# Pinning the first readers of the solved blocks behind the latest weights, and writing them ten units later

## The chip, the cores and the metric

The kernel runs on one core of a Trainium2 chip. The metric is the device time of one execution in microseconds (us); 2533.32 us is the median of three runs before the change (2533.11 to 2533.87).

## What is computed

Two transformer blocks over 256 tokens of width 2048, batch 1, all in float32. The first block has two mixers side by side: a gated delta rule (GDN, 8 heads of 128) and a block attention, which for 256 tokens is plain causal attention (8 heads of 128). Their outputs are gated, summed and projected, and a convolved gated feed-forward of width 5632 follows. The second block (two layers with modulation, sparse attention and retention) is not touched.

The change sits in the GDN. Cut to what matters, for each head:

```python
a_mat = where(strict, (k * beta) @ k.T * gamma, 0)     # per chunk of tokens
t_mat = triangular_solve(eye + a_mat, eye)             # unit lower triangular inverse
u = t_mat @ (v * beta)
w = t_mat @ (k * beta * exp(gc))
# scan over the chunks:
v_new = u - w @ state
o = (q * exp(gc)) @ state + (q @ k.T * gamma) @ v_new
state = state * exp(g_last) + kd.T @ v_new
```

The kernel uses two chunks of 128 tokens a head in place of the reference's chunks of 64, which gives the same output.

## The kernel before

**Weights.** All matrix products run in float32 split into a rounded high half and a low half (three matmuls a tile). Weights come in granules of 128 x 1024 (512 KB; 128 x 696 for the attention's value blocks). `load_w` (lines 215 to 227) issues the DMA of a granule on SP's queue (`w`, 4 buffers), rounds it on ACT into `wh` (line 222, 3 buffers) and takes the rest on DVE into `wl` (line 223, 4 buffers). A chunk of projection output (128 columns by 256 tokens) needs two granules, 48 matmuls. Between granules a side job issues a share of the modulation vector's products: a 256 KB DMA `mw` and one DVE instruction (line 1094), three for four granules.

**Who orders what.** TensorE's instructions run in the order in which the program writes them. For every other engine a planner fixes the order of its queue from priorities and its own cost estimates; each queue then runs strictly in that order. `behind()` (lines 230 to 234) is a means to hold the planner: what is written inside it comes, on its own engine, after the DMA, the ACT copy and the DVE subtraction of the granule loaded last.

**Tasks and the emission clock.** The work between the big products is written by generators (tasks). `self.clk` counts units of TensorE time: a matmul of 256 columns in the rounded format adds 0.107, one in plain float32 four times as much per column. After each triplet of weight matmuls `tick` advances the first task in the list whose time has come by one step; `yield 3.0` means "not before 3 units from now". `finish(t)` writes steps, always of the task that is due first, and moves the clock forward to it, until t is done: no weight matmuls come between these steps.

**The GDN.** Heads go in two groups of four. Per group (`mixers`, lines 589 to 628):
- key and query chunks of each head (`kq`, two buffers) and a task `gdn_scores`, which writes the head's blocks into a tile `gS`, two heads to a tile, three tiles in all;
- one task `gdn_solve` (line 785) once all four score tasks are done: POOL issues four DMAs that gather the 32 x 32 diagonal blocks in DRAM (`gD`, line 799), reads them as 32 partitions of 32 x 32 (`gX`, line 800), eliminates 30 columns with two POOL instructions each (lines 805 and 806), stores `gX`, and issues eight DMAs that put the blocks back into `gS` (line 810). The task yields 1.3 units a column and 8 after the last DMA, then sets `group.solved`;
- value and gate chunks, then a task `gdn` (line 814) for each head. It polls once a unit until `group.solved`; heads 2 and 3 of a group also wait for heads 0 and 1. Its first step reads the solved blocks on DVE (`level(0)`: `gbm`, line 829, and `DE`, line 834); 3.5 units later TensorE transposes `DE` (line 838); then two merging levels, the products with the values, the norm and the gate follow in about ten steps.

Forced finishes in group 1: heads 0 and 1 of group 0 are finished after the key and query chunks of head 6, since its tile `gS` is theirs (line 602). After group 1 come a value block of the attention (`a_block(2)`) and eight attention heads of two chunks each; the attention task of head h - 2 is finished before the chunks of head h (line 633).

Of the kernel before, what the change touches and what calls it, by code (L numbers as in the profile page):

```python
# [12 lines left out]
OP = mybir.AluOpType  # L13
# [24 lines left out]
def _consts():  # L38
# [37 lines left out]
    ret = {"rot": rot}  # L76
    dec = np.ascontiguousarray((dec * SC).astype(f).transpose(1, 0, 2, 3)).reshape(H, P, 2 * P)
    return base, gdn, ret, dec, lev


# [45 lines left out]
class Net:  # L126
# [386 lines left out]
    def mixers(self, bo, b1):  # L513
        nc, tmp, a = self.nc, self.tmp, self.a
        self.b1 = b1
        raw = self.side("v")
        ln1 = lambda k: self.col("ln1", k)

        def prep(k):
            if k == 1:  # L520
                nc.sync.dma_start(self.xg[0][:, 1:4], a["xT"][:, 1:4])
            if k == 8:
                nc.sync.dma_start(self.par[:, KT:], a["par"][:, KT:])
            if k % 4 == 2 and k < 12:
                g = k // 4 + 1
                nc.sync.dma_start(self.xg[g], a["xT"][:, 4 * g:4 * g + 4])
            if k == 12:
                nc.sync.dma_start(self.cst0, a["cst0"])
                nc.sync.dma_start(self.mod, a["bmod"])
                nc.sync.dma_start(self.row, a["row"].to_broadcast([P, 272]))  # L530
            self.raw(raw[k], k, ln1)
            self.sumsq(self.acc, self.x[k], k == 0)

        hs = self.side("u")
        nrm = {}

        vb = [b1.tile([P, 1024], F32, name=f"vb{tt}") for tt in range(2)]

        def a_block(b, scale):
            ps = self.gemm_a(a["wA1"][b], NA1, hs if b else raw, None if b else prep)  # L540
            if b == 0:
                nrm["task"] = self.add(self.normalize(0.0, [self.acc], self.one_norm, hs, ln1, out=nrm))
                while "col" not in nrm:
                    self.step(nrm["task"])
                scale = nrm["col"]
                self.add(self.gdn_gates(ps, scale))
            lo = b * NA1
            j0, j1 = max(lo, 16), min(lo + NA1, 1040)
            for tt in range(2):
                d, q = vb[tt][:, j0 - 16:j1 - 16], ps[tt][:, j0 - lo:j1 - lo]  # L550
                if b == 0:
                    nc.scalar.mul(d, q, scale[:, tt:tt + 1])
                else:
                    nc.scalar.copy(d, q)

        a_block(0, None)
        self.cst1 = b1.tile([P, CST1.shape[1]], F32, name="cst1")
        nc.sync.dma_start(self.cst1, a["cst1"])
        lev = self.pw.tile([P, 1024], F32, tag="w", name="levf", bufs=4)
        nc.sync.dma_start(lev[:, 0:3 * P], a["lev"])  # L560
        self.lev = b1.tile([P, 3 * P], mybir.dt.bfloat16, name="lev")
        nc.vector.tensor_copy(self.lev, lev[:, 0:3 * P])
        self.bo, self.hs = bo, hs
        self.mod_done, self.mod_ahead, self.pmo = 0, [], None
        self.job("mod", self.modulation(), 0)
        ci = 0

        def early():

            nonlocal ci  # L570
            ps = self.chunk(a["wB1"][ci], raw if ci < NRAW else hs)
            ci += 1
            if ci > NRAW:
                return ps
            t = tmp.tile([P, T], F32, tag="rt1", name="un", bufs=2)
            nc.vector.tensor_tensor(t, ps, nrm["row"][:, 0:T], op=OP.mult)
            return t

        def part(dst, j, h):
            ps = early()  # L580
            if j < 3:
                self.conv(dst, ps, lambda t: self.col("gconv", (j * 8 + h) * 4 + t), 4)
            nc.scalar.activation(dst, dst if j < 3 else ps, ACT.Silu)
            if ci == NRAW:
                self.finish(nrm["task"])
                o = self.side("v")
                self.oa, self.ob = o[0:8], o[8:16]

        groups = []
        for p in range(2):  # L590
            hh = range(4 * p, 4 * p + 4)
            group = Group(hh)
            S = []
            for i, h in enumerate(hh):
                kq = b1.tile([P, 2, T], F32, tag="kq", name="kq", bufs=2)
                for j, dst in ((1, kq[:, 0]), (0, kq[:, 1])):
                    part(dst, j, h)
                if i >= 2:
                    self.finish(group.scores[i - 2])
                if i % 2 == 0:  # L600
                    if p and i:
                        for t in groups[0].heads[:2]:
                            self.finish(t)
                    S.append(b1.tile([P, 2, 6, P], F32, tag="gS", name="gS", bufs=3))
                group.scores.append(self.add(self.gdn_scores(h, kq, S[i // 2][:, i % 2], group)))
            group.solve = self.add(self.gdn_solve(S, group))
            for i, h in enumerate(hh):
                v = b1.tile([P, T], F32, tag="v", name="v", bufs=1)
                if p and i >= 1:
                    self.finish(groups[0].heads[i - 1])  # L610
                z = b1.tile([P, T], F32, tag="z", name="z", bufs=5)
                part(v, 2, h)
                part(z, 3, h)
                if i >= 1:
                    self.finish(group.values[i - 1])
                group.values.append(self.add(self.gdn_values(h, v, group.scores[i], group)))
                group.z[h] = z
                if (p, i) == (0, 0):
                    self.mod_to(bo, RATE[0])
                if (p, i) == (0, 3):  # L620
                    with self.behind():
                        posf = self.pos_row(tmp, a["positions"], "sq")
                        cos, sin = self.trig(b1, posf, self.c1("rope"), "rope")
                    a_block(1, None)
            for i, h in enumerate(hh):
                group.heads.append(self.add(self.gdn(h, S[i // 2][:, i % 2], group, group.heads[i - 2:i - 1] if i >= 2 else
                                                     groups[-1].heads[2 + i:3 + i] if groups else [])))
            groups.append(group)
        a_block(2, None)
        mob = []  # L630
        for h in range(H):
            if h >= 2:
                self.finish(mob[h - 2])
            qk = b1.tile([P, 2, T], F32, tag="kq", name="qkb", bufs=2)
            for j in range(2):
                ps = self.chunk(a["wB1"][ci], hs)
                ci += 1
                self.rotate(qk[:, j], ps, cos, sin, 32)
            mob.append(self.add(self.moba(h, qk[:, 0], qk[:, 1], vb, self.ob[h])))
        self.mod_to(None, 0)  # L640
        self.sig = [self.gates(m) for m in range(4)]
        self.drain()
# [142 lines left out]
    def gdn_solve(self, S, group):  # L785


        nc, b1 = self.nc, self.b1
# [19 lines left out]
        nc.gpsimd.dma_start(Df, X)  # L808
        for d, y in diag:
            nc.gpsimd.dma_start(y, d)  # L810
        yield 8.0
        group.solved = True

    def gdn(self, h, S, group, before):
        nc, b1 = self.nc, self.b1
# [8 lines left out]
        idb = self.c0("ident").unsqueeze(1).to_broadcast([P, 2, P])  # L824

        def level(l):
            m = self.lev[:, l * P:(l + 1) * P].unsqueeze(1).to_broadcast([P, 2, P])
            bm = tl("bm", [P, 2, P])
            nc.vector.tensor_tensor(bm, B, m, op=OP.mult)
            return bm  # L830

        bm = level(0)
        DE = tl("DE", [P, 2, 2, P])
        nc.vector.tensor_tensor(DE[:, 1], idb, bm, op=OP.subtract)
        yield 3.5
        pd = self.aux([P, 2, P])
        for tt in range(2):
# [2 lines left out]
        for l in (1, 2):  # L840
            bm = level(l)
# [630 lines left out]
```

## Time and profile before

| what | value |
|---|---|
| median of three runs | 2533.32 us |
| profiled execution, its own time | 2533.55 us |
| its span | 2531.7 us |
| TensorE busy | 2454.0 us (97%), 20026 matmuls |
| DVE busy | 1905.9 us (75%) |
| ACT busy | 1391.4 us (55%) |
| POOL busy | 140.6 us (6%) |
| memory traffic, mean | 212 GB/s |

Busy TensorE time counts pipelined matmuls, so a share of 97% is no peak; where TensorE does not reach 9 tenths in a slice, something kept it waiting. The page's slices are 63 us each. The work spoken of here lies between 50 and 480 us.

### The profile page before, as it was taken

The page shows a single profiled execution, that of the slowest core. Times are in us where ns is not written, and L with a number is a line of the kernel's source. Part 1 is how long each engine was busy: PE and PEld are TensorE (multiplying, and loading weights), DVE is VectorE, ACT ScalarE, POOL GpSimd, SP SyncE. Part 2 cuts the span into 40 slices and gives each one's busy share as a digit, 9 for nine tenths or more (in the row PEclk, how much of TensorE's full clock was granted, in tenths as well). Part 3 has the DMA queues.
Part 4 walks back from the last instruction along what each step waited for, and adds up shares of the span by engine and source line. Part 5 has one row for each costly group of instructions (what it writes and reads, how often), then busy time and mean ns, then how long its engine had stood idle before and what let it go on. Part 6 is the DMA issues. An engine that isn't in the chain of part 4 may idle for free.

```text
span 2531.7 us, 50856 instructions
## 1 busy us (share of the span) xinstructions
PE 2454.0 (97%) x20026; PEld 2438.4 (96%) x20026; DVE 1905.9 (75%) x3673; ACT 1391.4 (55%) x2208; POOL 140.6 (6%) x215
## 2 busy tenths in 40 slices
PE   8959779999999999999999999999999999999999
PEld 8959779999999999999999999999999999999999
DVE  7747567667788988888877678898888677666664
ACT  7626446544444556777754456654844556475443
POOL 0341610000000000000000000000000000000000
PEclk9979989999999999999999999999999999999999
DMA  6545474588898766766767767768677555455555
GB/s 219 192 148 168 137 229 143 183 266 300 295 299 297 225 223 209 239 221 210 243 215 211 242 216 218 216 211 266 211 245 236 179 183 174 152 169 171 176 184 159
DMA packets 190224, 536.66 MB, mean 212 GB/s; under 512 B 22176, under 2 KB 27680, under 8 KB 189984
## 3 DMA queue, kind: packets, MB, share of 16 engines
q1 hardware_dynamic: 188768, 532.36, 65.5%
q8 instruction: 157, 2.57, 0.4%
q0 software_dynamic: 1216, 1.05, 0.2%
q14 instruction: 83, 0.68, 0.1%
HBM read 530.70 MB, written 2.62 MB: 211 GB/s over the span
## 4 chain that ended last, share of the span: by engine, by line
PE 89%; DVE 3%; POOL 3%; DMA 2%; issue 1%; ACT 1%; SPq 0%; DVEq 0%; ACTq 0%; POOLq 0%
PE mm L186 84%; PE aux L186 4%; POOL gX L806 2%; POOL gXt L805 1%; DVE wl L223 1%; PE aux L190 1%; ACT wh L222 1%; DVE mw L1094 0%; DVE isc L1304 0%; DMA gX<-gD 0%; DMA w<-wA 0%; DMA gD<-gS 0%; DMA mc<-c 0%; DMA gD<-gX 0%; DMA mw<-wM 0%
## 5 line engine op out<-in xcount | busy, mean ns | idle before, releaser
L222 ACT CAST wh<-w 128x1024 fp32r<-128x1024 f32 (+5 forms) x867 | 854.0, 986 | 938.0 <-PE mm L186 771.4
L186 PE MATMUL mm<-u,wh 128*128 128x256 f32 (+1 forms) x7488 | 1361.9, 284 | 0.0
L223 DVE TENSOR_TENSOR wl<-w,wh 128x1024 fp32r<-128x1024 f32 (+5 forms) x867 | 993.6, 1147 | 400.6 <-ACT wh L222 396.1
L186 PEld LDWEIGHTS mm<-u,wh 128*128 128x128 f32 x7488 | 1152.8, 189 | 3.3 <-issue 2.4
L186 PE MATMUL mm<-u,wl 128*128 128x256 f32 (+1 forms) x3744 | 1053.9, 281 | 51.7 <-DVE wl L223 51.7
L186 PEld LDWEIGHTS mm<-u,wl 128*128 128x128 f32 x3744 | 706.9, 189 | 52.1 <-DVE wl L223 52.1
L186 PE MATMUL mm<-v,wh 128*128 128x256 f32 (+1 forms) x4096 | 743.4, 283 | 0.0
L186 PEld LDWEIGHTS mm<-v,wh 128*128 128x128 f32 x4096 | 629.3, 189 | 1.4 <-issue 1.0
L186 PE MATMUL mm<-v,wl 128*128 128x256 f32 (+1 forms) x2048 | 576.2, 281 | 1.6 <-DVE wl L223 1.4
L186 PEld LDWEIGHTS mm<-v,wl 128*128 128x128 f32 x2048 | 385.8, 188 | 2.6 <-DVE wl L223 2.6
L1094 DVE CUSTOM_DVE_ANT_0 mw<-mw,mc,mod 128x512 f32<-128x512 f32 x192 | 145.0, 759 | 2.9 <-ACT mc L1076 2.1
L1094 DVE CUSTOM_DVE_ANT_0 mw<-mw,mc,part 128x512 f32<-128x512 f32 x192 | 142.2, 747 | 2.7 <-ACT mc L1076 2.7
L186 PE MATMUL mm<-wh,u 128*128 128x412 f32 (+1 forms) x320 | 83.4, 339 | 0.0
L1052 ACT ACTIVATE leaf<-bit,row,dr 128x384 f32<-128x384 f32 x120 | 78.9, 699 | 0.0
L186 PE MATMUL mm<-wh,v 128*128 128x412 f32 (+1 forms) x256 | 71.8, 359 | 5.7 <-ACT wh L222 5.7
L694 DVE SCALAR_TENSOR_TENSOR u<-mm,par,u 128x255 f32<-128x255 f32 (+1 forms) x160 | 76.4, 477 | 0.7
L335 POOL TENSOR_TENSOR rc<-rc,cst 128x2 f32<-128x2 f32 x4 | 3.7, 928 | 1296.2 <-DVE rc L388 1296.2
L186 PE MATMUL mm<-more,wh 128*128 128x256 f32 x384 | 69.8, 281 | 0.0
L186 PEld LDWEIGHTS mm<-more,wh 128*128 128x128 f32 x384 | 59.1, 189 | 0.0
L186 PEld LDWEIGHTS mm<-wh,u 128*128 128x128 f32 x320 | 58.3, 188 | 0.2
L186 PEld LDWEIGHTS mm<-wh,v 128*128 128x128 f32 x256 | 50.2, 200 | 6.8 <-ACT wh L222 6.6
L1056 DVE COPY_PREDICATED leaf<-bit,leaf 128x384 f32<-128x384 uint32 x88 | 53.5, 608 | 2.5 <-ACT leaf L1052 1.9
(297 smaller groups left out, 1996.2 us busy)
## 6 DMA issues: line engine op xcount, KB each, us to landing
w<-wB SPq DMA_DIRECT2D x344, 512.0 KB, 3.9
mw<-wM SPq DMA_DIRECT2D x384, 256.0 KB, 4.0
w<-wUp SPq DMA_DIRECT2D x170, 512.0 KB, 4.0
w<-wO SPq DMA_DIRECT2D x96, 512.0 KB, 4.2
w<-wDn SPq DMA_DIRECT2D x64, 384.0 KB, 3.6
w<-wDn SPq DMA_DIRECT2D x64, 320.0 KB, 3.5
w<-wA SPq DMA_DIRECT2D x48, 412.0 KB, 3.2
w<-wBr SPq DMA_DIRECT2D x32, 512.0 KB, 4.4
```

Of the source, the lines that this page charges most:

```text
L186: self.nc.tensor.matmul(out, l, r, start=start, stop=stop)
L190: self.nc.tensor.transpose(out, in_, self.c0("ident"))
L222: i1 = nc.scalar.copy(h[:, :n], w[:, :n])
L223: i2 = nc.vector.tensor_tensor(l[:, :n], w[:, :n], h[:, :n].bitcast(F32), op=OP.subtract)
L335: self.nc.gpsimd.tensor_tensor(out, in_, e, op=OP.pow)
L694: nc.vector.scalar_tensor_tensor(dst[:, s:], ps[:, :T - s], tap(width - 1 - s), dst[:, s:], op0=OP.mult, op1=OP.add)
L805: nc.gpsimd.tensor_tensor(t, col, row, op=OP.mult)
L806: nc.gpsimd.tensor_tensor(X[:, 0:j, j + 1:32], X[:, 0:j, j + 1:32], t, op=OP.subtract)
L1052: nc.scalar.activation(t, bits[0], ACT.Identity, scale=dr[:, i, h:h + 1], bias=rb[:, i, 0, h:h + 1])
L1056: nc.vector.copy_predicated(t, bits[l].bitcast(mybir.dt.uint32), u)
L1094: self.nc.vector.tensor_tensor_reduce(w, w, c, 1.0, src, OP.mult, OP.add, dst)
```

## The change

Three edits. The wait after the solve's last DMA grows from 8 to 18 units of the emission clock. The two DVE instructions of `level(0)` are written inside `behind()`. The finish of the score task of two heads earlier moves ahead of a head's `kq` tile and chunks, and is done for every head from the third on, across the two groups (before: after the chunks, for the third and fourth head of a group).

```diff
             for i, h in enumerate(hh):
+                if h >= 2:
+                    self.finish((groups + [group])[(h - 2) // 4].scores[(h - 2) % 4])
                 kq = b1.tile([P, 2, T], F32, tag="kq", name="kq", bufs=2)
                 for j, dst in ((1, kq[:, 0]), (0, kq[:, 1])):
                     part(dst, j, h)
-                if i >= 2:
-                    self.finish(group.scores[i - 2])
                 if i % 2 == 0:
...
         for d, y in diag:
             nc.gpsimd.dma_start(y, d)
-        yield 8.0
+        yield 18.0
         group.solved = True
...
-        bm = level(0)
         DE = tl("DE", [P, 2, 2, P])
-        nc.vector.tensor_tensor(DE[:, 1], idb, bm, op=OP.subtract)
+        with self.behind():
+            bm = level(0)
+            nc.vector.tensor_tensor(DE[:, 1], idb, bm, op=OP.subtract)
         yield 3.5
```

## Rows read from the trace of the kernel before

**Rows 1.** The page, busy tenths and granted clock in 40 slices of the span

```profile
PE   8959779999999999999999999999999999999999
PEclk9979989999999999999999999999999999999999
```

**Rows 2.** TensorE's waits, 0 to 420 us: total us, times, longest

```profile
PE mm L186 <- DVE wl L223: 53.4, 5, 26.4
```

**Rows 3.** Stretches: PE, PEld, DVE, ACT, POOL busy us; clock; DMA share; GB/s

```profile
134.67:161.06 26.39, 0.00 (x1) 0.01 (x1) 2.63 (x6) 0.45 (x1) 19.76 (x39) 0.54 0.05 10
161.06:165.00 3.94, 3.94 (x21) 3.94 (x22) 3.94 (x14) 0.18 (x1) 0.00 (x0) 0.61 0.48 157
165.00:181.50 16.50, 16.05 (x101) 15.54 (x100) 13.14 (x25) 9.01 (x16) 0.00 (x0) 1.00 0.82 266
...
225.25:234.09 8.84, 6.08 (x42) 4.58 (x40) 5.65 (x21) 6.19 (x19) 2.37 (x3) 1.00 0.38 124
...
303.20:328.51 25.31, 0.05 (x1) 0.00 (x0) 2.62 (x6) 0.87 (x2) 18.71 (x38) 0.58 0.06 10
...
374.90:385.00 10.10, 8.05 (x60) 7.09 (x59) 8.19 (x28) 6.86 (x20) 0.00 (x0) 1.00 0.45 148
```

**Rows 4.** Timeline of DVE: start, us, instruction, idle before and its releaser

```profile
158.43 0.76 DVE L829 TENSOR_TENSOR gbm<-gS,lev 128x256 f32<-128x256 f32 x2 [29.16 <-DMA gS<-gD]
159.78 1.22 DVE L223 TENSOR_TENSOR wl<-w,wh 128x1024 fp32r<-128x1024 f32 x1
...
188.40 1.23 DVE L223 TENSOR_TENSOR wl<-w,wh 128x1024 fp32r<-128x1024 f32 x1 [0.94 <-ACT wh L222]
...
325.89 0.76 DVE L829 TENSOR_TENSOR gbm<-gS,lev 128x256 f32<-128x256 f32 x2 [27.96 <-DMA gS<-gD]
```

**Rows 5.** Timeline of TensorE: weight matmuls behind the stall and later

```profile
161.43 0.63 PE L186 MATMUL mm<-u,wh 128*128 128x256 f32 x2
...
181.55 0.39 PE L186 MATMUL mm<-u,wh 128*128 128x256 f32 x2
...
181.90 0.40 PE L186 MATMUL mm<-u,wh 128*128 128x256 f32 x2
```

**Rows 6.** Timeline of POOL: the solve of group 0

```profile
109.81 0.87 POOL L805 TENSOR_TENSOR gXt<-gX 32x30 f32<-32x30 f32 x1 [3.92 <-DMA gX<-gD]
...
127.20 1.52 POOL L806 TENSOR_TENSOR gX<-gX,gXt 32x220 f32<-32x220 f32 x1
...
130.49 0.60 POOL L805 TENSOR_TENSOR gXt<-gX 32x234 f32<-32x234 f32 x1
...
138.92 0.59 POOL L805 TENSOR_TENSOR gXt<-gX 32x228 f32<-32x228 f32 x1
...
140.98 0.60 POOL L806 TENSOR_TENSOR gX<-gX,gXt 32x220 f32<-32x220 f32 x1
...
151.56 0.25 POOL L806 TENSOR_TENSOR gX<-gX,gXt 32x30 f32<-32x30 f32 x1
```

**Rows 7.** DMAs to landing: those of tile gX, then those of gS

```profile
DMA to landing us min/median/max: 2.3/3.3/4.4
...
DMA to landing us min/median/max: 1.7/1.9/3.7
```

**Rows 8.** Timeline of TensorE: GDN and attention steps

```profile
202.89 0.38 PE L190 MATMUL aux<-cst,gDE 128*128 128x128 f32 x2
...
205.13 0.95 PE L186 MATMUL aux<-cst,gsq 128*128 128x1 f32 x8
...
370.38 0.38 PE L190 MATMUL aux<-cst,gDE 128*128 128x128 f32 x2
...
374.91 0.82 PE L186 MATMUL aux<-qkb 128*128 128x128 f32 x4
...
442.43 0.82 PE L186 MATMUL aux<-qkb 128*128 128x128 f32 x4
...
451.29 1.65 PE L186 MATMUL aux<-spt,vb 128*128 128x128 f32 x6 [1.64 <-ACT spt L919]
```

## The prediction

> **What bounds the kernel now.** Read the 40 slices of the page first: TensorE is at 9 tenths almost everywhere, and the exceptions lie in the first 440 us, slices 3, 5 and 6 above all, with the granted clock down in the third and the sixth [rows 1]. The waits of TensorE in that stretch come next: one line holds nearly all of them, 53.4 us for the low halves of weights (wl, line 223), the longest 26.4 us [rows 2]. The stretches place it: TensorE does nothing in 134.67 to 161.06 and in 303.20 to 328.51, DVE next to nothing, while POOL works on [rows 3]. Then ask DVE what it stands at: line 829, the first reader of the solved blocks, idle 29.16 and 27.96 us until the DMA that writes the blocks back lands; the next wl runs only behind it [rows 4]. So these two stretches are bound by the solve on POOL, and only because a reader stands in DVE's queue ahead of weights that need nothing from it. The first TensorE work on that reader's result is at 202.89 and 370.38, more than 40 us later in the stream [rows 8]: nobody needs it where it stands.
>
> **The change, part by part.** Sums are against the profiled execution, 2533.55 us (its span 2531.7 and 1.85 around it), 0.23 over the median.
>
> *The pin.* Lines 829 and 834 at level 0 go behind the wl of the granule latest loaded when they are written. Where is that? The write of level 0 lies 3.5 units of the emission clock ahead of the transposes; a unit is 1.12 us of TensorE (a triplet of 256 columns counts 0.32 and takes 0.358, the step from 181.55 to 181.90 [rows 5]). So it lies at 202.89 - 3.9 = 199.0 and at 370.38 - 3.9 = 366.5. The pinned pair can't reach the wl of 134.67 or 303.20 any more. The level 1 reader writes the same buffer (gbm, one copy), so it stays behind line 834 without a pin. Both stalls go: 26.39 + 25.26 = 51.65 us. With them goes the slow restart: after 161 a triplet takes 0.64 instead of 0.358 at a granted clock of 0.61 [rows 3, 5], about 1.4 us until 164 (0.25 for the first, four at 0.28) and as much is taken after 328.5; and 0.45 us of idle at 165, where the window has 16.05 busy of 16.50. Gain: 51.65 + 2.8 + 0.45 = 54.9 us.
>
> *What is late next: the solve itself.* DVE was idle for the second half of it and won't be now. Twelve rounds beside a working DVE took 109.81 to 130.49, 20.7 us; the mirrored twelve, of the same sizes, beside an idle one 138.92 to 151.81, 12.9 us; the same 220-element subtraction is 1.52 and 0.60 [rows 6]. The ratio is 1.60. The 18 rounds left at 130.49 (21.3 us) become 34.2 and end at 164.7, in the denser attention block (DVE 80% busy at 165 to 181.5 [rows 3]) perhaps at 167. From there to the landed blocks it was 6.6 us (151.81 to 158.4); with both transfers at their slowest (4.4 for 2.3, 3.7 for 1.9 [rows 7]) 10.5. The blocks land between 171 and 178.
>
> The Trainium skill (SBUF — State Buffer, section Who interferes with whom) says that a DVE instruction with two SBUF inputs and a GpSimd instruction that reads SBUF exclude each other for a whole instruction; by that, with wl and modulation products both of that kind and DVE at 80%, the solve would crawl at a fifth of its speed until DVE stands still again. The trace agrees with the lock for single instructions (1.52 for 0.60), not with that share: 1.60 was measured beside a normal stream. Its result is the second rival.
>
> *The 18 for 8.* Ten units later is 11.2 us of TensorE: the write moves from 199.0 to about 210 and from 366.5 to 377.7 in the old stream. In both groups a forced finish comes first. For group 0 the head-6 block begins at about 204.8 (the squares of head 4's scores, 205.13, now stand there too [rows 8]); the moved finish of head 4's scores jumps the emission clock by 2.5 units and adds 2.4 us of score matmuls that exist anyway. So level 0 is written at 205 to 208. Less the 28.2 us gained, that is 177 to 180 in real time. DVE makes a wl 4.6 us ahead of its use (188.40 for the fifth granule from 181.55, four of 2.87 us later [rows 4, 5]), so it can be at the pinned pair at 170, wait up to 8 us, and needs 1.35 (158.43 to 159.78) and 1.15 more for the next wl, due at 179.0 behind the score matmuls. With a landing at 171 nothing is lost, at 178 1.5 us. Group 1's solve lies 167.5 us behind (325.89 less 158.43 [rows 4]), so it would land at 338 to 346, where the finish of 374.9 begins at 348.2 (less its own stall and restart, 26.7). I take 1 us for both, bounds 0 and 5. With 8 left in place level 0 would be written at 170.8 and a landing at 178 would come up to 8 us late; the 18 covers the stretched solve.
>
> *What 18 costs.* Heads 0 and 1 must be done before head 6's blocks are allotted, and that place doesn't move. Already now this finish runs bare, without weights between: 225.25 to 234.09 with 2.76 us idle [rows 3]. The chain starts some 7 units later (10, less the jump), so four more of its steps fall into the bare stretch. A step of two heads costs about 1.8 us in such a stretch (the five and a half steps of 374.90 to 385.00), 7.2 us; their 24 matmuls, which are merely moved, take 0.134 each (8.05 us for 60 [rows 3]), 3.2. That leaves 4 us, bounds 1 (other scores fill it) and 8. In group 1 the finish of the first attention head (374.9) runs beside heads 4 and 5 and has 2.05 us idle in 10.1 [rows 3]. With 18 these heads only begin there. An attention head with little beside it needs 442.43 to 451.29 plus 0.8, 9.7 us from its scores to its last product [rows 8]; with 17 matmuls of attention and only 12 of heads 4 and 5 to fill it, 29 at 0.134 or 3.9 us, 5.8 are idle: 4 us more than now (3.75), bounds 1 and 7. The later heads 6 and 7 fall beside attention heads that idle 1.64 us at 451 anyway [rows 8]; I count nothing, at most 2 us back.
>
> *The moved finish.* It issues no new instruction, no DMA; scores come some microseconds earlier, and cover is the head-6 weights already three granules ahead. Nothing; bounds -1 and +2. The SP queue is passed by nothing. POOL keeps its order: the powers of the next heads' scores queue behind the solve, and their readers come 40 us later.
>
> *DVE while the solve runs.* The attention block at 137 to 153 will run beside POOL. After the stall the same block took DVE 13.14 of 16.50 us with POOL idle [rows 3]; if its instructions grow by a quarter beside POOL, it is as long as TensorE's work, and beyond that it is the bound. No row shows this block so. At POOL's own ratio, 1.60, it would be 21.0 us, 4.5 too long; a lead of 4.6 us stands against that. 1 us, bounds 0 and 4.5.
>
> Sum: 2533.55 - 54.9 + 1 + 4 + 4 + 1 = **2489** (2488.7).
>
> **Rivals.** *Chains stay covered (2481).* The bare stretches cost 1 and 1 instead of 4 and 4, the landing and DVE's extra nothing: 2488.7 - 6 - 2. For it: POOL, ACT and DVE have nothing else to serve in a bare stretch, so a step may be shorter. Against: the finishes do not move.
>
> *The solve lands late (2507).* POOL gets only the gaps of DVE. It limits itself: where DVE stops at the pinned pair at 170, POOL is fast again. If the 39.5 us from 130.49 to 170 gave it a quarter (DVE is 80% busy in the denser window [rows 3]), they do 10 of the 21.3 us, 11.3 are left at 170, plus 8 to land: landing at 189.3, next wl at 191.8, 13 us late, and 6 to 13 in group 1 where the bare stretch hides some; about 18.5 in all above the forecast. Against it stands the 1.60.
>
> *The stalls stay (2533).* If something else in front of the weights reads the blocks, or the planner leaves the pair where it is. Against: only lines 829 read them on DVE, and the wait is theirs alone [rows 4].
>
> *Slower (up to 2566).* One mechanism: bare finishes everywhere. While heads wait for the solve, four of them poll once a unit, and a unit has 3.1 turns, so scores and attention tasks, which stand behind them, get none and are written in finishes, without weights. If all four pairs (ten steps, 18 us less 8 of own work, 10 idle each) and all eight attention finishes (5.8 each) ran so, that is 86, 80 more than now (2.76 + 2.05 + 1.64), in place of the forecast's 8: 2488.7 + 72 = 2560, and with heads 4 to 7 drained bare behind the last attention head some 6 more. It is slower than before from about two thirds of that on. For it: the polling grows by 10 units. Against: it ends with the solve, and only the first pair of each group has a finish close behind it.
>
> **How the numbers follow.** Forecast 0.60 (its own range 2483 to 2498); chains covered 0.17; late solve 0.15; stalls stay 0.04; slower 0.04. The range 2480 to 2507 holds the first, most of the second and half of the third, 0.84. A change under 0.2% (5 us) can't be told from none. Faster by more: 0.60 + 0.17 + 0.15 = 0.92, and a little from partial cases, 0.93; within 0.03; slower 0.04.
>
> **What would show it.** Right: no wait of TensorE on wl over 3 us before 440 us; line 829 idle under 8 us; the late rounds of the solve at some 1.6 times their old length; a clock digit of 9 in every slice to 440 us; idle of TensorE just behind head 6's first blocks and behind the second attention head, 8 and 6 us. Wrong: line 829 idle over 12 us with wl behind it (late solve), the two old stalls in place, or bare stretches of over 20 us.

## Result: faster by 1.1%, two thirds of the forecast gain

The changed kernel takes 2504.94 us (median of four, 2503.77 to 2507.96) against 2533.22 us for the kernel before beside it: a ratio of 0.9891, interval 0.9874 to 0.9908, or 28.3 us. The profiled execution took 2503.77 us, 29.8 less than the one of before. The forecast was 2489 us, 44.9 less than its own base of 2533.55, with a range of 2480 to 2507: direction and range hold, a third of the gain is missing.

The page of the changed kernel, to be read against [rows 1]: slices 3, 5 and 6 have filled up to 8, 9 and 9 tenths, but slice 4 has fallen from 9 to 8.

```profile
PE   8988999999999999999999999999999999999999
...
PEclk9998999999999999999999999999999999999999
```

TensorE's waits of the changed kernel from 0 to 420 us (total us, times, longest). The row of [rows 2] has gone from 53.4 to 2.0; a new one, on the squares of fresh scores (gsq, line 736), is on top.

```profile
PE aux L186 <- ACT gsq L736: 14.3, 4, 10.8
...
PE aux L190 <- ACT gR L893: 6.3, 3, 3.0
...
PE mm L186 <- DVE wl L223: 2.0, 3, 1.1
```

**A ledger.** Both kernels issue the same matmuls, so the same piece of work can be found in both traces and the difference in its start tells what has been won so far. Work between 93 and 130 us comes 1.3 us later than before. The first value block of the attention starts at 138.45 instead of 165.13, 26.7 earlier: the first stall gave 28.0. Its end is 26.0 earlier (0.7 lost). The last transposes of heads 0 and 1 come 9.7 earlier (16.2 lost), the values of group 1 5.5 earlier (4.2 lost). The second value block starts 32.2 earlier, so the second stall gave 26.7; the attention keeps 29.7 of it (2.5 lost). Won 54.7, lost 24.9.

Two windows of each trace show what kind of loss it is: columns as in [rows 3], the changed kernel first, then the same work before.

```profile
138.45:155.41 16.96, 16.29 (x99) 15.29 (x98) 16.54 (x23) 8.72 (x15) 15.71 (x17) 1.00 0.74 243
155.41:224.15 68.74, 52.85 (x397) 49.27 (x395) 45.62 (x95) 32.89 (x63) 22.73 (x31) 0.90 0.53 175
224.15:271.73 47.58, 44.21 (x333) 42.34 (x333) 28.35 (x67) 26.26 (x54) 8.12 (x14) 0.93 0.41 127
...
318.47:400.00 81.53, 75.22 (x629) 73.88 (x629) 61.65 (x154) 48.40 (x114) 14.48 (x22) 1.00 0.58 190
```

```profile
181.39:233.89 52.50, 49.07 (x396) 46.83 (x395) 39.36 (x82) 33.00 (x59) 3.40 (x4) 1.00 0.65 216
233.89:277.26 43.37, 40.99 (x333) 39.41 (x334) 30.02 (x71) 25.38 (x57) 8.65 (x14) 1.00 0.41 131
...
350.67:429.70 79.03, 75.16 (x622) 73.50 (x622) 57.03 (x143) 47.32 (x113) 2.88 (x4) 1.00 0.55 184
```

With some 396 matmuls on either side, TensorE's idle time in the first pair goes from 3.43 (52.50 less 49.07) to 15.89 us, and its busy time from 49.07 to 52.85 at a mean granted clock of 0.90: 12.5 of idle and 3.8 of slow matmuls. In the second pair it is 1.0 and 3.2.

**Where the 12.5 sit.** TensorE in the changed kernel, 178 to 225 us:

```profile
178.66 0.95 PE L186 MATMUL aux<-cst,gsq 128*128 128x1 f32 x8
179.47 0.90 PE L186 MATMUL aux<-cst,g 128*128 128x128 f32 x4
191.13 1.86 PE L186 MATMUL aux<-cst,gsq 128*128 128x1 f32 x8 [10.76 <-ACT gsq L736]
192.86 1.63 PE L186 MATMUL aux<-cst,g 128*128 128x128 f32 x4
...
196.70 0.58 PE L186 MATMUL mm<-u,wh 128*128 128x256 f32 x2
...
223.04 0.58 PE L190 MATMUL aux<-cst,gR 128*128 128x128 f32 x2 [3.02 <-ACT gR L893]
```

At 178.66 the moved finish writes the first step of head 4's scores. What comes next is not head 4's second step but the first step of head 5's scores (191.13): the finish writes whatever task is due first, and head 5's had become due. Followed step by step through the program, the squares of both heads are written in the finish at the same count of the emission clock: head 4's because the polling heads had taken every turn until then, head 5's because its task had just been added. Both steps on TensorE are due 4 units later, one behind the other, and head 4's second step is due no sooner than 2.5 units after its first. Head 5's key and query had only just left TensorE. Between them no weight matmul stands, so TensorE idles 10.76 us and then runs at half clock (1.2 GHz; the granted clock is 0.50 from 191.13 to 194.50): 1.86 where the same eight took 0.95.

DVE and ACT say why the squares took so long: DVE first, then ACT, changed kernel.

```profile
178.91 0.76 DVE L829 TENSOR_TENSOR gbm<-gS,lev 128x256 f32<-128x256 f32 x2 [5.47 <-DMA gS<-gD]
...
180.25 0.48 DVE L694 SCALAR_TENSOR_TENSOR kq<-mm,par,kq 128x255 f32<-128x255 f32 x1
...
188.16 0.47 DVE L694 SCALAR_TENSOR_TENSOR kq<-mm,par,kq 128x253 f32<-128x253 f32 x1
```

```profile
183.07 0.42 ACT L583 ACTIVATE kq<-kq 128x256 f32<-128x256 f32 x1 [6.13 <-DVE kq L694]
...
190.45 0.63 ACT L736 ACTIVATE gsq<-kq 128x512 f32<-128x512 f32 x1
```

Line 829, pinned, stood 5.47 us at the landing DMA, and behind it in DVE's queue stood the convolutions of head 5's key (180.25 on). The weights were covered, as forecast (wl waits of 1.1 at most); the scores that the finish called for were not.

POOL's solve of group 0 in the changed kernel, to be read against [rows 6]:

```profile
132.71 0.93 POOL L805 TENSOR_TENSOR gXt<-gX 32x234 f32<-32x234 f32 x1
...
147.25 1.13 POOL L806 TENSOR_TENSOR gX<-gX,gXt 32x220 f32<-32x220 f32 x1
...
167.72 0.26 POOL L806 TENSOR_TENSOR gX<-gX,gXt 32x30 f32<-32x30 f32 x1
```

The 18 rounds after the middle take 35.3 us (132.71 to 167.98); the forecast had 34.2. From there to DVE's start at 178.91 it is 10.9 us.

### The profile page after: what moved, and what is told of

It reads as the page before. It is cut to its first block, busy times and chain, and to the rows that moved or that the text cites. A ratio compares the mean times of both kernels' runs of the same rounds, so it can differ in the third digit from the quotient of the medians.

```text
span 2502.0 us, 50870 instructions
## 1 busy us (share of the span) xinstructions
PE 2457.6 (98%) x20026; PEld 2440.8 (98%) x20026; DVE 1920.7 (77%) x3673; ACT 1392.0 (56%) x2208; POOL 169.6 (7%) x215
## 4 chain that ended last, share of the span: by engine, by line
PE 88%; POOL 5%; DVE 3%; issue 2%; DMA 2%; ACT 1%; SPq 0%; DVEq 0%; POOLq 0%; ACTq 0%
PE mm L186 83%; PE aux L186 4%; POOL gX L806 2%; POOL gXt L805 2%; DVE wl L223 1%; PE aux L190 1%; DMA gX<-gD 0%; DMA gD<-gX 0%; DVE isc L1305 0%; DVE mw L1095 0%; DMA gS<-gD 0%; ACT wh L222 0%; DMA w<-wA 0%; DVE kq L694 0%; DMA gD<-gS 0%
## 5 line engine op out<-in xcount | busy, mean ns | idle before, releaser
L1095 DVE CUSTOM_DVE_ANT_0 mw<-mw,mc,mod 128x512 f32<-128x512 f32 x192 | 151.3, 792 | 3.8 <-ACT mc L1077 3.7
```

Source lines behind the costliest of these rows:

```text
L1095: self.nc.vector.tensor_tensor_reduce(w, w, c, 1.0, src, OP.mult, OP.add, dst)
```

## Experiments

Theory A: the pin carries the gain, and the finish in its new place gives some 10 us back because it writes other tasks' steps. The rivals put the loss on the 18 units (bare steps of the heads) or on the landing, whatever the finish does. The kernel before ran beside the experiments at 2534.35 us (the first three and the one without the pin), 2534.98 us (the next four) and 2535.30 us (the last group).

**The pin alone** (8 units and the finish as before):

```diff
-        bm = level(0)
...
-        nc.vector.tensor_tensor(DE[:, 1], idb, bm, op=OP.subtract)
+        with self.behind():
+            bm = level(0)
+            nc.vector.tensor_tensor(DE[:, 1], idb, bm, op=OP.subtract)
```

> The kernel before with the pin alone: 8 units, the finish in its old place. Theory A (the pin removes the stalls; what was lost behind it comes from the moved finish, which writes the next head's fresh scores bare): the pair is now pinned where level 0 is written at 199.0 of the old stream, 171 in real time; DVE reaches it at about 165 and waits until the blocks land at 178, the next wl is ready at 180.5 against a due time of 173.5: 7 us idle of TensorE and about 1 us of slow restart in group 0, about 6 + 1 in group 1, and no bare wait for gsq. 2533.5 - 54.9 + 15 + 1 = 2495, faster than the full change by 8 to 10 us. Theory B (the 18 is what takes the stalls away, the pin alone leaves most of them): TensorE still waits 20 us or more for wl twice, 2515 to 2530.

Measured: 2495.28 us, 0.9843 (0.9828 to 0.9858). One edit of three gives 39 us, some 11 more than all three. TensorE's longer waits in it, from two stretches of its timeline:

```profile
180.67 0.58 PE L186 MATMUL mm<-u,wl 128*128 128x256 f32 x1 [5.44 <-DVE wl L223]
...
327.20 0.39 PE L186 MATMUL mm<-u,wl 128*128 128x256 f32 x1 [2.82 <-DVE wl L223]
...
338.01 1.23 PE L186 MATMUL aux<-gDE,gbm 128*128 128x128 f32 x4 [4.13 <-ACT gDE L840]
```

With 8 units the landing does reach TensorE, through wl, by 8.3 us in all. It is still the better bargain.

**The finish restricted to its own task** (everything else as changed):

```diff
+    def alone(self, t):
+        while not t.done:
+            self.clk = max(self.clk, t.ready)
+            self.step(t)
...
-                    self.finish((groups + [group])[(h - 2) // 4].scores[(h - 2) % 4])
+                    self.alone((groups + [group])[(h - 2) // 4].scores[(h - 2) % 4])
```

> The full change, but the moved finish steps only the score task it is for, and no other task that is due meanwhile. Theory A (the finish pulls the next head's score step, whose squares are not there yet: 10.8 us idle and 3 us at the low clock): that wait goes, but level 0 of heads 0 and 1 is written later, since the clock no longer jumps past the solve's 18 units, so about five more chain steps run bare before head 6's tile: -14 + 5, about 2495. Theory C (it is the DVE wait for the landed blocks that holds TensorE up there, through the convolution queued behind it): the idle stays at some 8 to 10 us under another name, 2503 to 2508. Theory D (the late start of the head chains is what costs): slower than the full change, 2510 or more.

Measured: 2496.37 us, 0.9846 (0.9831 to 0.9861), an interval that does not touch the changed kernel's. Its TensorE at the same place:

```profile
178.18 0.95 PE L186 MATMUL aux<-cst,gsq 128*128 128x1 f32 x8
178.99 0.90 PE L186 MATMUL aux<-cst,g 128*128 128x128 f32 x4
179.73 1.47 PE L186 MATMUL aux<-kq 128*128 128x512 f32 x6
...
190.19 1.05 PE L186 MATMUL aux<-cst,gsq 128*128 128x1 f32 x8 [0.73 <-ACT gsq L736]
```

Head 4's second step follows its first, weights come in between, and head 5's scores wait 0.73 us in place of 10.76. Place and number of units are those of the changed kernel; only whose steps are written differs. That is the cause of most of the shortfall, shown by taking it away. DVE's reader of the blocks stood at the landing here too, 4.08 us in group 0, while TensorE's waits on wl are 1.8 us in all.

**The same with 14 units**:

```diff
-        yield 18.0
+        yield 14.0
```

> As the run with only its own steps, with 14 units in place of 18, so that level 0 is written about one granule behind its place in the full change: the pull of the fresh scores is taken away and the start of the head chains nearly kept. Theory A: 10.8 us idle and 3 us of low clock go, 1 to 3 us of later chain come, 2504.9 - 12 = 2493. Theory C (the wait for the landing): DVE still waits some 3 to 5 us at line 829, and TensorE as long behind it: 2500 to 2503. Theory D (late chains): between the run with 18 and the full change.

Measured: 2492.56 us, 0.9836 (0.9820 to 0.9853), the lowest median of all; its interval overlaps that of the pin alone, so no more than equal is shown. DVE's wait for the blocks in it, between 100 and 440 us, and DVE's wait in group 0 in a second execution of the same kernel (from the last group below):

```profile
DVE gbm L829 <- DMA gS<-gD: 10.4, 2, 6.8
```

```profile
179.53 0.43 DVE L829 TENSOR_TENSOR gbm<-gS,lev 128x256 f32<-128x256 f32 x1 [5.21 <-DMA gS<-gD]
```

The 10.4 us (6.7 in the changed kernel) are mostly group 1's; where the changed kernel loses its time, in group 0, the first execution has only 3.59. The second has 5.21, nearly the changed kernel's 5.47, and TensorE's waits on wl are 2.3 us in all and its longest on gsq 2.1. So DVE's wait at the landing does not by itself hold TensorE with 14 or 18 units, and the rival that put the loss on the landing, whatever the finish does, falls.

**Without the pin** (18 units and the moved finish):

```diff
-        with self.behind():
-            bm = level(0)
-            nc.vector.tensor_tensor(DE[:, 1], idb, bm, op=OP.subtract)
+        bm = level(0)
...
+        nc.vector.tensor_tensor(DE[:, 1], idb, bm, op=OP.subtract)
```

> The full change without the pin: 18 units and the moved finish stay. Theory A (only the pin moves the readers in DVE's queue; the other two edits only cost): the planner leaves the pair ahead of the wl of 134.67 and of 303.20, both stalls of 25 to 26 us stay, and the bare stretch before head 6 costs some 8 to 12 us more than before (the landing is long past, so less than the 16 of the full change): 2540 to 2546. Theory B (the 18 moves the readers): the stalls shrink by 10 units, 11 us each, 2510 to 2520.

Measured: 2551.81 us, 1.0066 (1.0051 to 1.0081), 17 us slower than before; the expectation had 6 to 12. TensorE's largest waits, 0 to 420 us, and one row of its timeline:

```profile
PE mm L186 <- DVE wl L223: 52.1, 4, 27.0
PE aux L186 <- ACT gsq L736: 9.6, 4, 6.1
```

```profile
212.24 1.87 PE L186 MATMUL aux<-cst,gsq 128*128 128x1 f32 x8 [6.07 <-ACT gsq L736]
```

Both stalls are back, so later emission by itself moves no reader in DVE's queue. The finish calls for head 5's scores here too (212.24), long after the blocks have landed: the chain from fresh key and query to squares costs 6.1 us alone, so some 4.7 of the changed kernel's 10.76 are the landing's (the last group below has more on this). Matched weight by weight with the kernel before, the profiled execution has lost 11.3 us by the last transposes of heads 0 and 1, within the 8 to 12 expected of that stretch; some 4 more are lost up to the second stall and some 3 in the attention, and these are not explained.

**The moved finish alone** (8 units, no pin):

```diff
+                if h >= 2:
+                    self.finish((groups + [group])[(h - 2) // 4].scores[(h - 2) % 4])
...
-                if i >= 2:
-                    self.finish(group.scores[i - 2])
```

> The kernel before with the moved finish alone: 8 units, no pin. Theory A (the moved finish costs through the 18: only with it do four polling heads keep head 4's first score step back until the finish, which then runs past head 5's): with 8 that step is written before the finish, no fresh squares are pulled, the wait for gsq stays at about 3 us in all: 0 to 3 us above before, 2534 to 2537. Theory A2 (the moved finish costs by itself): the 10 to 14 us of the bare stretch show here too, 2544 to 2548.

Measured: 2538.40 us, 1.0011 (1.0002 to 1.0021), 2.8 us slower by the ratio. By itself the edit costs little more than the +2 that the forecast had as its bound. Its price comes up together with the 18: ten more units of four polling heads keep head 4's scores from being stepped until the finish, and by then head 5's are due as well. With 8, followed through the program, head 4's squares are written before the finish, and its steps come due ahead of head 5's. Its longest wait on gsq is 2.1 us.

**Pin and 18, finish in its old place**:

```diff
-                if h >= 2:
-                    self.finish((groups + [group])[(h - 2) // 4].scores[(h - 2) % 4])
...
+                if i >= 2:
+                    self.finish(group.scores[i - 2])
```

> The full change with the finish in its old place: pin and 18 units. Theory A: the wait for gsq goes and nothing is pulled, but heads 0 and 1 begin only in the second chunk of head 6, and nearly their whole chain runs bare with head 4's and 5's scores: some eight steps, 14 us less 5 of own work, 9 idle and 2 of low clock, against 3.4 idle now; no wait for the landing in group 0. 2504.9 - 14 + 6 = 2497. Theory D (the late start of the chains is the main cost): above the full change, over 2505.

Measured: 2496.99 us, 0.9847 (0.9831 to 0.9862). So the 18 costs next to nothing over the 8 of the pin alone: TensorE's wait on wl falls from 10.1 to 2.1 us, and about as much comes up in other places, on an attention head's rotated queries and keys (qkb) above all. Rows of both, TensorE's waits from 0 to 420 us, the pin alone first:

```profile
PE mm L186 <- DVE wl L223: 10.1, 5, 5.4
...
PE aux L186 <- ACT gDE L840: 4.1, 1, 4.1
```

```profile
PE aux L186 <- DVE qkb L466: 9.0, 2, 6.0
...
PE mm L186 <- DVE wl L223: 2.1, 3, 1.1
```

The rival that put the loss on the 18 falls. The moved finish on top of these two edits costs the rest: 0.9891 less 0.9847 is 11 us.

**Pin and 12 units, finish in its old place** (edit against the pin alone):

```diff
-        yield 8.0
+        yield 12.0
```

> The pin alone with 12 units in place of 8, the finish in its old place. The pin alone took 2495.3 and still had 5.4 and 2.8 us of waits on wl behind the landing, 4.1 on gDE and a slow restart. Four units later is 4.5 us: theory A says that most of these 10 to 12 us go and 2 to 4 come back in the bare stretch before head 6: 2487 to 2490, the fastest of all. If the landing is not what these waits hang on: 2494 to 2499.

Measured: 2495.32 us, 0.9846 (0.9830 to 0.9861): a miss, nothing gained over the 8. The waits on wl did fall, to 5.1 us in all, and the time went elsewhere. Two of its TensorE waits and two windows:

```profile
PE aux L190 <- ACT gR L893: 6.0, 3, 2.7
...
PE aux L186 <- ACT gDE L840: 5.0, 1, 5.0
```

```profile
180.00:220.00 40.00, 33.72 (x238) 31.50 (x239) 27.67 (x69) 20.10 (x47) 6.25 (x8) 0.91 0.40 127
320.00:340.00 20.00, 14.29 (x103) 13.65 (x102) 13.69 (x31) 10.07 (x18) 4.41 (x8) 0.87 0.68 217
```

What the landing no longer takes from the weights, the heads' own chains take in the bare stretches behind it (gR, gDE), and these windows run at a mean granted clock of 0.91 and 0.87.

**24 units** (everything else as changed):

```diff
-        yield 18.0
+        yield 24.0
```

> The full change with 24 units in place of 18: the pull of head 5's scores stays, the wait of DVE for the landed blocks goes. Theory A (the wait for gsq is the pull, about 6 us of it, and the landing, about 5): the 10.8 us shrink to about 6, and the head chains start six units later, 3 to 5 us more idle before head 6's tile: 2502 to 2506. Theory C (the landing is the whole of it): the wait goes below 2 us, 2494 to 2498.

Measured: 2505.44 us, 0.9881 (0.9866 to 0.9895), the changed kernel's time. TensorE's two longest waits:

```profile
186.87 1.87 PE L186 MATMUL aux<-cst,gsq 128*128 128x1 f32 x8 [7.55 <-ACT gsq L736]
...
345.31 1.62 PE L186 MATMUL aux<-qkb 128*128 128x128 f32 x4 [9.49 <-ACT mS L910]
```

DVE's wait in group 0:

```profile
180.04 0.43 DVE L829 TENSOR_TENSOR gbm<-gS,lev 128x256 f32<-128x256 f32 x1 [2.22 <-DMA gS<-gD]
```

The longer delay does not end the call for head 5's scores, and it does not end DVE's wait at the landing, as expected, but leaves 2.22 us of it; without these the 7.55 is 5.3. That the delay shortens the call is not shown: an unaltered execution of the changed kernel had 7.87 (below). In group 1 a finish of an attention head now runs bare for 9.49 us: what the forecast feared of the 18 happens at 24.

**Unaltered kernels once more**: the changed kernel twice, and the two best versions in more rounds. The question was what an execution's own chance does, above all for the 1.3 us lost by 93 us.

> The changed kernel, unaltered, profiled again. In its profile the clock is 0.92 at 79 to 100 us and head 3's scores come 15.2 us after head 2's; in the kernel before it is 1.00 and 13.7 us, after the same wait of 2.07 us. Theory E (an execution's chance): a second profile of the same kernel can show 1.00 and 13.7; and the low clock behind the wait of 2.7 us at 268 us can come or go as well. Theory F (something in the edits brings the low clock): 0.92 and 15.2 again, and the low clock at 268 to 272 us again. Under both the wait of 10.8 us for the squares of head 5 stays, within 1 us, since it lies in the order of the work. Time 2503 to 2508 us.

> The changed kernel, unaltered, a third profile. Theory E: any of the two clocks at 79 to 100 us, and this profile may differ from the one before it. Theory F: 0.92 at 79 to 100 us in this one too. Under both the wait for head 5's squares is 10 to 11.5 us. Time 2503 to 2508 us.

> The changed kernel with the finish restricted to its own task's steps and 14 units, timed in more rounds beside the pin alone. If its lower median (2492.6 against 2495.3 us) is more than the spread of executions, the ratio is 0.983 to 0.984 with an interval below 0.985; if it is spread, the two kernels come out within 0.001 of each other. I expect 0.9838. At 79 to 100 us its first profile had a clock of 1.00; by theory E this one may have 0.92, by theory F it has 1.00.

> The pin alone in more rounds: 0.9845, 2495 us. At 79 to 100 us its first profile had a clock of 0.92; by theory E this one may have 1.00, by theory F it has 0.92. TensorE's waits on wl, 5.4 and 2.8 us in its first profile, come again within 1.5 us under both.

Measured: the changed kernel 2502.82 and 2510.90 us, both outside the 2503 to 2508 expected; its own steps with 14 units 2492.70 us, 0.9830 (0.9817 to 0.9844); the pin alone 2493.54 us, 0.9833 (0.9820 to 0.9847). No difference between the two is shown; the pin alone is the smaller change. Its waits on wl behind the landings were 3.40 and 3.78 us where 5.4 and 2.8 had been expected within 1.5: the first is a miss.

The window of 79 to 100 us bears on the 1.3 us. It is the pin alone, its first execution and then its second:

```profile
79.00:100.00 21.00, 21.00 (x152) 19.83 (x152) 10.99 (x23) 11.51 (x19) 2.20 (x2) 0.92 0.44 155
```

```profile
79.00:100.00 21.00, 20.22 (x157) 19.05 (x157) 12.02 (x24) 13.10 (x21) 2.21 (x2) 1.00 0.49 173
```

One kernel has both clocks behind the same wait of 2.06 us, and head 3's scores come 15.2 or 13.7 us after head 2's. The changed kernel showed 0.92 three times, the one with 14 units 1.00 twice; of all fourteen profiles six have 0.92. So this loss needs no edit, and theory E holds for the pin alone; for the changed kernel it is likely and not shown. At 250 to 275 us E shows nothing: the clock is 0.93 in all three executions of the changed kernel and in both of the pin alone, 1.00 in both of the one with 14 units; there it goes with the kernel.

The wait for head 5's squares came at 7.87 and 11.54 us beside the first 10.76, a wider spread than the 1 us expected, and the spread is instructive. DVE's line 829 and the squares' matmul on TensorE, second execution and then third:

```profile
175.08 0.76 DVE L829 TENSOR_TENSOR gbm<-gS,lev 128x256 f32<-128x256 f32 x2 [2.33 <-DMA gS<-gD]
```

```profile
187.30 1.87 PE L186 MATMUL aux<-cst,gsq 128*128 128x1 f32 x8 [7.87 <-ACT gsq L736]
```

```profile
179.41 0.76 DVE L829 TENSOR_TENSOR gbm<-gS,lev 128x256 f32<-128x256 f32 x2 [6.21 <-DMA gS<-gD]
```

```profile
191.65 1.87 PE L186 MATMUL aux<-cst,gsq 128*128 128x1 f32 x8 [11.54 <-ACT gsq L736]
```

From DVE's start at line 829 to the squares' matmul it is 12.22, 12.24 and, in the first execution, 12.22 us (191.13 less 178.91). DVE stood 2.33, 6.21 and 5.47 us at the landing; taken off the idle time that leaves 5.5, 5.3 and 5.3, near the 5.3 of the kernel with 24 units and the 6.07 of the one without the pin. So the idle time is a chain of 5 to 6 us, which the finish calls for, and the landing on top of it, microsecond for microsecond. Of the 8.1 us between the second and the third execution some 4 lie here and some 3.5 at the finish of the first attention head in group 1; the latter are not explained.

## Why the prediction was right in direction and short in size

- *The pin*: forecast 54.9, measured 54.7 (28.0 and 26.7). Right, with its reason: the pin alone ends the stalls, and without it they stay.
- *The solve and the landing*: the rounds took 35.3 us for 34.2 forecast, from a start 2.2 us later than [rows 6] has it; the end, 168, is a microsecond past the forecast's 167, and the way to DVE's start was 10.9 us against 10.5 with both transfers slow. So DVE started at 178.91, just past the 171 to 178 (175.08 and 179.41 in the other executions), and idled 5.47, under the 8 named; in group 1 it started at 337.11, 158.2 us behind group 0 where the forecast took over 167.5 from the old stream, and idled 1.20. The Trainium skill (SBUF — State Buffer, section Who interferes with whom) has a DVE instruction with two SBUF inputs and a GpSimd instruction that reads SBUF exclude each other. The solve that crawls beside a DVE 80% busy was the forecast's own working from that, and it did not come: in the value block DVE was 98% busy (16.54 of 16.96) and the solve kept its pace. The exclusion shows in single instructions (1.13 us where [rows 6] has 0.60 for an idle DVE) and not as the share of time that DVE leaves free. The forecast's 1 us for the landing was right for the weights, and wrong for the scores behind the same instruction.
- *What 18 costs*: forecast 4 and 4. The bare stretch of heads 0 and 1 has 4.95 us idle (0.74, 0.66, 3.02 and 0.53) against 2.76, so 2.2; the attention in group 1 lost 2.5. Both within the bounds; the 18 against the 8 with the pin (2496.99 and 2495.28) shows that what it costs is about what it saves at the landing: it gained nothing.
- *DVE while the solve runs*: forecast 1, measured 0.7.
- *The moved finish*: "It issues no new instruction, no DMA ... Nothing; bounds -1 and +2." This is the step that failed. Taken away, it gives 11 us (0.9891 against 0.9847, or against 0.9846 with only its own steps). In the profiled execution it is most of the 16.2 us of heads 0 and 1, where the sum had 5 (1 for the landing, 4 for the bare stretch): 10.76 idle, 4.7 to 5.5 of them by way of the landing, and 3.8 of slow matmuls. Cover was sought in the weights ahead, and that held. What wasn't asked is which task is due first when the finish runs, and whether its operands exist. The part on the 18 counted a jump of the clock by 2.5 units, as if head 4's squares stood already; the finish wrote them too, and passed the 4 units behind them, at which head 5's step was due as well. The text had the mechanism in hand, in the rival on the slower side: polling heads starve the scores, which "are written in finishes, without weights". It was priced there for every finish and at nothing for the one that the change moves.
- *Not in the sum at all*: 4.2 us between 224 and 272, most of it clock. TensorE in the changed kernel, then in the kernel before at the same work:

```profile
267.79 0.59 PE L190 MATMUL aux<-cst,gR 128*128 128x128 f32 x2 [2.72 <-ACT gR L893]
...
269.17 0.63 PE L186 MATMUL mm<-u,wh 128*128 128x256 f32 x2
```

```profile
275.05 0.59 PE L190 MATMUL aux<-cst,gR 128*128 128x128 f32 x2 [2.06 <-ACT gR L892]
...
276.19 0.40 PE L186 MATMUL mm<-u,wh 128*128 128x256 f32 x2
```

The last step of a pair of heads waits in both; in the changed kernel the matmuls behind it run 0.63 instead of 0.40 for 3 us. The pin alone has the low clock here too, so the finish is not its cause; what is stays open.

The 1.3 us by 93 us are the other term that the sum did not have, and they are most likely an execution's chance. With the measured terms the sum closes, as differences of one pair of traces must: 2533.55 - 54.7 + 1.3 + 0.7 + 16.2 + 4.2 + 2.5 = 2503.75, for 2503.77. Of the signs that the forecast named, the waits on wl (1.1 at most), line 829 (5.47) and the rounds (35.3 for 21.3, 1.66 times) came out; the clock digit of 9 in every slice did not, since slice 4 has 8. The late-solve rival names a time close to the measured one (2507), but by landings at 189 and waits on wl, and neither is there. That the range of 2480 to 2507 held the time is therefore luck: its upper part was kept for that rival, and the forecast's own range ended at 2498. What stays open as well: the forecast's terms without the moved finish still give 2489, and the best versions take 2493 to 2497.

## What to carry to other kernels

Before a forced finish is moved, write down which task is due first at its new place and when that task's operands exist: a helper that advances "whatever is due" can call for work that was emitted a moment ago, and then two whole chains run with nothing beside them. A reader that stands early in a strict queue is worth moving only as far as the first place where nobody behind it is urgent; look at all that stands behind it, not at the weights alone. In this kernel moving it 4 or 10 units further gained nothing (2495.32 and 2496.99 against 2495.28 us). And test a change of three edits by its parts: here one edit was worth some 39 us and the pair added to it took about 11 back.

## What the runs showed of the hardware that was not expected

- The same wait in the same kernel can be followed by either clock: behind 2.06 us before its matmuls at 78 to 80 us the pin alone ran on at 2.4 GHz in one execution and at 1.2 GHz for some 3 us in the other (1.00 and 0.92 over 21 us; a triplet of weight matmuls every 0.36 and every 0.64 us), which moves all that follows by 1.5 us. So a single execution can't tell gains of that size apart here, and a wait of 2.06 us can cost another 1.5 behind it.
- DVE's own instructions grew too beside POOL: the modulation product took 1.02 to 1.20 us in the value block while the solve ran and 0.74 to 0.75 behind it (at 172.68 and 187.49); the value block lost only 0.7 us by it.
